# Token sums and residual of a down projection, moved from VectorE and GpSimd to accumulating DMA

## The chip, the cores and the metric

The kernel runs on one core of one Trainium2 chip. The core has a matrix engine (PE), three elementwise engines (DVE, ACT, POOL), a queue engine (SP) and 16 DMA engines. The metric is the device time of one launch in microseconds. Plain loads and stores are issued from SP; transfers that add into their destination ("accumulating DMA") are issued from POOL.

## The reference, cut to what matters

A decoder trunk of two layers over 1024 tokens, model width 1024, everything in float32. Both layers end in a gated feed-forward block, and the change touches only that block's second half:

```python
def swiglu(h, w_gu, w_down):
    u = h @ w_gu
    g, v = u[..., :D_FF], u[..., D_FF:]          # D_FF = 2816
    return (jax.nn.silu(g) * v) @ w_down

h = h + swiglu(rmsnorm(h, norm_g[layer, 1]), ffn_w_gu[layer], ffn_w_down[layer])
```

The first layer's output feeds a key/value projection, the last layer's a final RMSNorm.

## The kernel before, in words

**Layout.** Activations lie transposed: model or hidden dimension in 128 partitions, the 1024 tokens along the row. A tile is 128x1024, "lo" is tokens 0 to 511 and "hi" tokens 512 to 1023. All large tiles come from one pool of 49 slots. A float32 product is made of three matmuls on split operands: ACT copies the operand to a rounded high part (`split`, L229) and DVE subtracts to get the low part (L230). Both parts share one tile, `so`.

**Down.** `ffn` writes 22 gated tiles `t1` to DRAM (`zd`). `down` multiplies them with the weights `w_dn` in `block_proj`, in three groups of 3, 4 and 4 pairs of tiles (`DG`). Inside a group the product of 2x2 blocks (two halves of the hidden dimension by two halves of the tokens) is done with seven block products instead of eight, as in Strassen's method. They are named j and run in the order 1, 5, 6, 3, 7, 4, 2; each has four output tiles p, and one (j, p) is 3 matmuls per pair of tiles: 9 in the first group, 12 in the others. A j is called a phase here, so a phase is 48 matmuls in groups two and three.

The operand X of a phase (`xop`, four tiles k in groups two and three) is a sum of quarters of the two stored tiles a = `raw[k]` and b = `raw[G+k]`. Before, the chain of sums runs in place on POOL: phase 5 takes a.hi - a.lo (L939), phase 6 takes b.hi minus that (L945), phase 7 a.hi - b.hi (L941), phase 4 takes b.lo minus the sum of phase 6 (L943). Each sum is then split by ACT and DVE into an `so` tile; phases 1 and 3 are split with a sign (L948, L949). The operand of the next phase is written into the program after the present phase's product of the same index.

The weights need such sums as well; those were already made by accumulating DMA (`acc`, L188, tile `wr`), each after the split that reads the old content.

Results leave PSUM (tiles pU, pV, pW) by a DVE add or subtract into the residual tiles `h` (L1018). These are loaded at the start of `down` from the DRAM copy `hd` with eight plain loads of 512 KB (L858).

**Order.** Apart from the recurrent layer, a scheduler sets the order of each engine's queue when the program is built; at run time every queue is strictly in order. Weight work runs ahead of the products by a fixed number of steps (`SLA` = 6 for splits, four more for the loads and sums).

Of the kernel before, what the change touches and what calls it, by code (L numbers as in the profile page):

```python
# [9 lines left out]
AF = mybir.ActivationFunctionType  # L10
ALU = mybir.AluOpType
# [4 lines left out]
KD = 8  # L16
# [3 lines left out]
DG = [3, 4, 4]  # L20
# [47 lines left out]
class Trunk:  # L68
# [602 lines left out]
    def ffn(self, L, h, last=False):  # L671
        nc = self.nc
        zd = self.dram(f"zd{L}", [FF_T, P, S])
        lo, hi = slice(0, 512), slice(512, 1024)
# [78 lines left out]

        banks, tmp = {}, {}

        def product(i):
            f, j = seq[i]
            bank, xn = prod[j]
            if (f, bank) not in banks:
                banks[(f, bank)] = self.ps("p" + bank)  # L760
            p = banks[(f, bank)]
            w = ops.pop((f, j))
            for k in range(4):
                wh, wl = w[:, k * P:(k + 1) * P], w[:, 512 + k * P:512 + (k + 1) * P]
                xh, xl = X[xn][k][:, lo], X[xn][k][:, hi]
                for n, (a, b) in enumerate(((wh, xh), (wh, xl), (wl, xh))):
                    nc.tensor.matmul(p, a, b, start=k + n == 0 and j in (1, 5, 6), stop=k == 3 and n == 2,  # L767
                                     skip_group_check=j not in (1, 5, 6))
# [3 lines left out]
        def evict(f, j):  # L772
            a, b, c = (banks.get((f, x)) for x in "abc")
            if j == 1:
                t0, t1, t2 = tmp[f] = [self.slot("ev") for _ in range(3)]
                nc.scalar.activation(t0[:, lo], a, AF.Copy)  # L776
                return
            t0, t1, t2 = tmp[f]
            rb = st.get("rb")
            if j == 6:  # L780
                V(t0[:, hi], t0[:, lo], b, ALU.subtract)
            elif j == 2:
                V(t2[:, lo], a, rb[:, lo], ALU.mult)
                nc.scalar.activation(t2[:, lo], t2[:, lo], AF.Silu)
                nc.gpsimd.tensor_tensor(t2[:, lo], t2[:, lo], rb[:, lo], ALU.mult)
            elif j == 7:
                V(t1[:, hi], b, t0[:, lo], ALU.subtract)
                V(t1[:, hi], t1[:, hi], c, ALU.add)
            elif j == 4:
                V(t1[:, lo], b, t0[:, lo], ALU.subtract)  # L790
                V(t1[:, lo], t1[:, lo], t2[:, lo], ALU.mult)
            elif j == 3:
                V(t0[:, hi], t0[:, hi], c, ALU.subtract)  # L793
                nc.gpsimd.tensor_tensor(t0[:, hi], t0[:, hi], rb[:, hi], ALU.mult)  # L794
                nc.scalar.activation(t0[:, hi], t0[:, hi], AF.Silu)  # L795
                nc.gpsimd.tensor_tensor(t0[:, hi], t0[:, hi], rb[:, hi], ALU.mult)
                V(t1[:, hi], t1[:, hi], t0[:, hi], ALU.mult)
                zout.append((f, t1))
                for x in "abc":
                    del banks[(f, x)]  # L800
                del tmp[f]
# [41 lines left out]
    def down(self, L, hd, zd, zout, last):  # L843
        nc = self.nc
        self.ld = 4
        for x in zout:
            nc.sync.dma_start(zd[x[0]], x[1])
        zout.clear()
        h = [None] * KD

        def zload(f):
            t = self.slot("zr")
            nc.sync.dma_start(t, zd[f])
            return t

        def hload(m):
            h[m] = self.slot("h")
            nc.sync.dma_start(h[m], hd[m])  # L858

        k0 = [2 * sum(DG[:g]) for g in range(len(DG))]  # L860
        pr = self.block_proj(h, hload, DG, [lambda k, g=g: zload(k0[g] + k) for g in range(len(DG))],
                             [f"d{L}_{g}" for g in range(len(DG))], [self.d["w_dn"][L, g] for g in range(len(DG))],
                             (1, 5, 6, 3, 7, 4, 2), last)
        next(pr)
        yield
        next(pr)
        yield
        next(pr)
        yield
        if last:  # L870
            st = {}

            def sq(m, c, eng):
                n = c.stop - c.start
                if c.start not in st:
# [12 lines left out]
        for j, p, c in pr:  # L888
            if last:
                for m, x in {3: ((p, hi),), 7: ((p + 4, hi),), 4: ((p + 4, q[0]), (p + 4, q[1]))}.get(j, ((p, c),) if c else ()):  # L890
                    with self.tc.high_priority(offset=PRIO if j == 2 else 0):
                        sq(m, x, nc.vector if j == 2 else nc.gpsimd)
                if (j, p) == (7, 3):
                    fin = self.finish(h, st.pop(512), 512, 512)
                if j == 4 or c == q[0]:
                    next(fin, None)
                if (j, p, c) == (2, 3, q[0]):
                    for _ in fin:
                        pass
                    fin = self.finish(h, st.pop(0), 0, 256)  # L900
                    with self.tc.high_priority(offset=PRIO):
                        next(fin)
            else:
                for m, x in {3: ((p, hi),), 7: ((p + 4, hi),), 4: ((p + 4, lo),), 2: ((p, lo),)}.get(j, ()):
                    kv(m, x)
                if (j, p) == (4, 3):
                    self.ld, self.sp = LD, SP
                    self.wpump(self.wi + 4, self.wi + 2)
        if last:
            next(fin)  # L910
            next(fin)
            f1 = self.finish(h, st.pop(256), 256, 256)
            with self.tc.high_priority(offset=PRIO):
                next(f1)
            for f in (fin, f1):
                for _ in f:
                    pass
            yield h
        else:
            yield kv  # L920

    def block_proj(self, h, hload, G, xload, wkey, wsrcs, order, tail=False):
        nc = self.nc
        V = nc.vector.tensor_tensor
        lo, hi = slice(0, 512), slice(512, 1024)
# [9 lines left out]
        def xop(g, j, k):  # L935
            a, b = xraw(g, k), xraw(g, G[g] + k)
            t = self.slot("so", F32R)
            if j == 5:
                nc.gpsimd.tensor_tensor(a[:, lo], a[:, hi], a[:, lo], ALU.subtract)  # L939
            elif j == 6:  # L940
                nc.gpsimd.tensor_tensor(a[:, lo], b[:, hi], a[:, lo], ALU.subtract)  # L941
            elif j == 4:
                nc.gpsimd.tensor_tensor(a[:, lo], b[:, lo], a[:, lo], ALU.subtract)  # L943
            elif j == 7:
                nc.gpsimd.tensor_tensor(a[:, hi], a[:, hi], b[:, hi], ALU.subtract)  # L945
            x = {1: a[:, lo], 2: b[:, lo], 5: a[:, lo], 6: a[:, lo], 3: b[:, hi], 7: a[:, hi], 4: a[:, lo]}[j]
            if j in (1, 3):
                nc.scalar.activation(t[:, lo], x, AF.Copy, scale=-1.0)  # L948
                nc.vector.scalar_tensor_tensor(t[:, hi], x, -1.0, t[:, lo].bitcast(F32),  # L949
                                               op0=ALU.mult, op1=ALU.subtract)  # L950
            else:
                self.split(t[:, lo], t[:, hi], x)
            X.setdefault((g, j), []).append(t)
            if j == order[6]:
                raw[g][k] = raw[g][G[g] + k] = None
# [44 lines left out]
        def product(i, c0=0, c1=512):  # L1000
# [14 lines left out]
            m += p  # L1015
            c = slice(c.start + c0, c.start + c1)
            with self.tc.high_priority(offset=PRIO if c1 - c0 < 512 else 0):
                V(h[m][:, c], h[m][:, c], ps, op)  # L1018
            if c1 < 512:
                return  # L1020
            del ops[i]
# [2 lines left out]
            if p == 3:  # L1024
                del X[(g, j)]

        moves = {1: (0, lo, ALU.subtract), 2: (0, lo, ALU.add), 5: (4, hi, ALU.add), 6: (0, hi, ALU.subtract),
                 3: (0, hi, ALU.subtract), 7: (4, hi, ALU.add), 4: (4, lo, ALU.add)}

# [17 lines left out]
        for i in range(len(seq)):  # L1047
# [4 lines left out]
            if tail and i >= len(seq) - 4:  # L1052
                product(i, 0, 256)
                yield j, p, slice(0, 256)
                continue
            product(i)
            ng, nj = (g, order[o + 1]) if o < 6 else (g + 1, order[0])
            if ng < len(G) and p < G[ng]:
                xop(ng, nj, p)
# [913 lines left out]
```

## Time and profile before

| | us |
|---|---|
| three runs | 2746.46, 2748.12, 2750.28 |
| the profiled execution, launch to end | 2747.98 |
| its span, first to last instruction | 2746.2 |
| PE busy in the span | 2660.8 (97%) |
| down of layer one, first to last product | 911.2 to 1134.4 |
| down of layer two, first product starts at | 2497.5 |

The profiled execution lies 0.14 us under the median of the runs, and 1.8 us of it lie outside the span. PE is busy nearly all the time at a granted clock of 0.985, so only the idle stretches of PE can be won without changing its work, and anything that makes PE wait is lost directly. In views by stretch, each engine's busy time and, in brackets, its instructions stand beside the granted clock, the busy share of the DMA engines and what they moved. A share a little over 1 is possible, since packets overlap.

### The profile page before, as it was taken

Reading aid. Unit: us, or ns where it says so; the run is one execution under the profiler, and the core shown is the slowest. Engines: PE = TensorE matmul, PEld = TensorE weight load, DVE = VectorE, ACT = ScalarE, POOL = GpSimd, SP = SyncE. Lnnn points to the kernel's source line nnn. Section 1 sums busy time; section 2 is a strip of 40 time slices with the busy share of each in tenths; the row PEclk is TensorE's granted clock in tenths of the full one; section 3 lists DMA queues with packets and bytes.
Section 4 is the critical chain, followed back from the end, with each engine's and each line's share of the span. In section 5 each row is a group of like instructions: output and inputs, shape, how many; then the busy total and the mean of one; then the engine's idle time right before and its main releaser. Section 6 shows DMA issues by size and latency. Waiting matters only on the chain.

```text
span 2746.2 us, 36684 instructions
## 1 busy us (share of the span) xinstructions
PE 2660.8 (97%) x12650; PEld 2207.8 (80%) x12650; DVE 1893.9 (69%) x3641; ACT 1294.6 (47%) x2500; POOL 1117.1 (41%) x1102
## 2 busy tenths in 40 slices
PE   8889999999999999999999999999999999999997
PEld 6668888788888788888888888888887888887786
DVE  7667533755555798647647999999856655557997
ACT  4667222432232443424515788999934323223433
POOL 1441002544343555110004677777734434336552
PEclk9989999999999999999999999999999999999998
DMA  3334243476664976352485322221254666659761
GB/s 121 91 99 151 98 152 102 106 176 152 163 150 116 311 200 137 130 153 84 163 240 158 82 68 66 66 67 58 95 182 104 168 161 150 150 134 280 195 150 62
DMA packets 175178, 377.03 MB, mean 137 GB/s; under 512 B 16896, under 2 KB 66432, under 8 KB 174992
## 3 DMA queue, kind: packets, MB, share of 16 engines
q1 hardware_dynamic: 121232, 256.79, 29.1%
q0 software_dynamic: 51872, 115.43, 20.1%
q8 instruction: 100, 1.64, 0.3%
q10 hardware_dynamic: 1888, 2.46, 0.3%
q14 instruction: 86, 0.70, 0.1%
HBM read 289.68 MB, written 78.64 MB: 134 GB/s over the span
## 4 chain that ended last, share of the span: by engine, by line
PE 59%; DVE 11%; issue 4%; DMA 3%; ACT 3%; POOL 1%; DVEq 0%; POOLq 0%; ACTq 0%
PE pb L767 12%; PE pc L767 8%; PE pa L767 7%; PE pn L237 7%; PE pU L1012 5%; PE psc L237 4%; PE pV L1012 3%; PE pt L1634 3%; DVE so L230 2%; DMA wr<-w_dn 2%; PE pwo L1824 2%; PE po L1672 1%; PE po L1673 1%; PE pW L1012 1%; DVE thl L230 1%
## 5 line engine op out<-in xcount | busy, mean ns | idle before, releaser
L230 DVE TENSOR_TENSOR so<-wr,so 128x512 fp32r<-128x512 f32 (+1 forms) x476 | 387.1, 842 | 58.5 <-ACT so L229 57.9
L229 ACT ACTIVATE so<-wr 128x512 fp32r<-128x512 f32 (+1 forms) x476 | 279.1, 611 | 255.4 <-DMA wr<-w_dn 115.1
L767 PE MATMUL pb<-so,so 128*128 128x512 f32 x1584 | 381.1, 391 | 1.9 <-DVE so L230 1.4
L767 PEld LDWEIGHTS pb<-so,so 128*128 128x128 f32 x1584 | 298.4, 189 | 64.9 <-DVE so L230 1.8
L767 PE MATMUL pa<-so,so 128*128 128x512 f32 x1056 | 254.4, 393 | 3.6 <-ACT ev L776 2.4
L767 PE MATMUL pc<-so,so 128*128 128x512 f32 x1056 | 255.6, 389 | 0.0
L188 POOL DMA_DIRECT2D wr<-w_gu x176 | 161.6, 1077 | 226.2 <-DVE so L230 177.1
L1012 PE MATMUL pU<-so,so 128*128 128x512 f32 x1056 | 245.3, 390 | 2.3 <-DVE so L230 2.3
L767 PEld LDWEIGHTS pa<-so,so 128*128 128x128 f32 x1056 | 199.9, 190 | 46.2 <-ACT ev L776 2.5
L237 PE MATMUL psc<-kl,ql 96*128 96x512 f32 (+2 forms) x960 | 234.6, 370 | 2.0 <-DVE thl L230 1.2
L1012 PEld LDWEIGHTS pU<-so,so 128*128 128x128 f32 x1056 | 197.8, 188 | 45.2 <-DVE so L230 3.9
L767 PEld LDWEIGHTS pc<-so,so 128*128 128x128 f32 x1056 | 198.3, 188 | 41.1
L795 ACT ACTIVATE ev<-ev 128x512 f32<-128x512 f32 x44 | 27.8, 633 | 345.7 <-POOL ev L794 345.7
L237 PEld LDWEIGHTS psc<-kl,ql 96*128 96x128 f32 x960 | 165.7, 192 | 24.4 <-PE pt L1634 2.3
L188 POOL DMA_DIRECT2D wr<-w_dn x96 | 92.3, 1145 | 137.4 <-DVE so L230 67.6
L794 POOL TENSOR_TENSOR ev<-ev,rb 128x512 f32<-128x512 f32 x44 | 58.1, 1321 | 208.0 <-DVE ev L793 208.0
L230 DVE TENSOR_TENSOR thl<-pt,thl 128x512 fp32r<-128x512 f32 x198 | 133.0, 680 | 9.9 <-ACT thl L229 9.7
L1012 PE MATMUL pV<-so,so 128*128 128x512 f32 x528 | 125.9, 395 | 8.1 <-DVE so L230 6.9
L230 DVE TENSOR_TENSOR wl<-wr,wh 128x1024 fp32r<-128x1024 f32 (+4 forms) x79 | 89.2, 1145 | 55.1 <-ACT wh L229 31.2
L1012 PEld LDWEIGHTS pV<-so,so 128*128 128x128 f32 x528 | 99.5, 190 | 32.6 <-DVE so L230 8.8
L229 ACT ACTIVATE wh<-wr 128x1024 fp32r<-128x1024 f32 (+4 forms) x97 | 90.4, 956 | 74.0 <-DMA wr<-w_q 19.0
L229 ACT ACTIVATE thl<-pt 128x512 fp32r<-128x512 f32 x198 | 114.6, 598 | 21.1 <-PE pt L1634 19.3
(331 smaller groups left out, 6366.2 us busy)
## 6 DMA issues: line engine op xcount, KB each, us to landing
wr<-w_gu SPq DMA_DIRECT2D x110, 512.0 KB, 5.0
wr<-w_gu POOLq DMA_DIRECT2D x176, 256.0 KB, 5.2
zd<-ev SPq DMA_DIRECT2D x44, 512.0 KB, 3.2
zr<-zd SPq DMA_DIRECT2D x44, 512.0 KB, 6.3
wr<-w_dn SPq DMA_DIRECT2D x40, 512.0 KB, 7.2
wr<-w_dn POOLq DMA_DIRECT2D x64, 256.0 KB, 5.6
ql<-qd SPq DMA_DIRECT2D x64, 192.0 KB, 3.0
wr<-w_in SPq DMA_DIRECT2D x23, 512.0 KB, 4.3
```

Of the source, the lines that this page charges most:

```text
L188: self.nc.gpsimd.dma_start(dst, src, accum_op=ALU.add)
L229: nc.scalar.activation(hi, src, AF.Copy)
L230: (nc.gpsimd if pool else nc.vector).tensor_tensor(lo, src, hi.bitcast(F32), ALU.subtract)
L237: self.nc.tensor.matmul(ps, a, b, start=j == 0, stop=j == n - 1)
L767: nc.tensor.matmul(p, a, b, start=k + n == 0 and j in (1, 5, 6), stop=k == 3 and n == 2, skip_group_check=j not in (1, 5, 6))
L794: nc.gpsimd.tensor_tensor(t0[:, hi], t0[:, hi], rb[:, hi], ALU.mult)
L795: nc.scalar.activation(t0[:, hi], t0[:, hi], AF.Silu)
L1012: nc.tensor.matmul(ps, a, b, start=k + n == 0 and j in (1, 5, 2), stop=k == G[g] - 1 and n == 2, skip_group_check=j not in (1, 5, 2))
L1634: nc.tensor.transpose(pt[:, h * P:(h + 1) * P], Pt[n][h][r][:, off:off + P], self.ident)
L1672: nc.tensor.matmul(po[n], v, thl[:, 0:512], start=False, stop=False)
L1673: nc.tensor.matmul(po[n], v, thl[:, 512:1024], start=False, stop=end)
L1824: self.nc.tensor.matmul(p, wk[a], x[b], start=k + j == 0, stop=k == KD - 1 and j == 2)
```

## The change

1. The four results that are the first to reach a quarter of `h` (phases 1, 5, 6 and 4 of the first group, 16 products per layer) are copied out of PSUM by ACT with the right sign, instead of being added by DVE to a loaded residual. The eight loads of `hd` go away.
2. The residual is added in the second group by 16 accumulating DMAs of 256 KB from `hd` into `h`, written into the program after the products of phases 6, 3, 4 and 2.
3. `ffn` stores its gated tiles with signs chosen so that every sum of `xop` is a plain addition. Two evictions per tile swap operands or an add for a subtract; their number is the same.
4. The token sums are then accumulating DMAs from `zd` into the loaded tile, each issued after the split that reads the old content. In groups two and three all four sums of a pair are DMAs. In the first group those of phases 5 and 6 stay on POOL and two are DMAs. Per layer, 44 POOL sums become 6, and 38 accumulating DMAs of 256 KB are added.

```diff
         def hload(m):
             h[m] = self.slot("h")
-            nc.sync.dma_start(h[m], hd[m])
+
+        def hadd(m, c):
+            self.acc(h[m][:, c], hd[m][:, c])
...
             t = self.slot("so", F32R)
-            if j == 5:
-                nc.gpsimd.tensor_tensor(a[:, lo], a[:, hi], a[:, lo], ALU.subtract)
-            elif j == 6:
-                nc.gpsimd.tensor_tensor(a[:, lo], b[:, hi], a[:, lo], ALU.subtract)
-            elif j == 4:
-                nc.gpsimd.tensor_tensor(a[:, lo], b[:, lo], a[:, lo], ALU.subtract)
-            elif j == 7:
-                nc.gpsimd.tensor_tensor(a[:, hi], a[:, hi], b[:, hi], ALU.subtract)
-            x = {1: a[:, lo], 2: b[:, lo], 5: a[:, lo], 6: a[:, lo], 3: b[:, hi], 7: a[:, hi], 4: a[:, lo]}[j]
-            if j in (1, 3):
+            s, c = {1: (a, lo), 2: (b, lo), 3: (b, hi), 7: (a, hi)}.get(j, (a, lo))
+            x = s[:, c]
+            if g == 0 and j in (5, 6):
+                nc.gpsimd.tensor_tensor(x, x, (a if j == 5 else b)[:, hi], ALU.add)
+            if j == 6:
                 nc.scalar.activation(t[:, lo], x, AF.Copy, scale=-1.0)
...
+            sa, sb = xsrc[g](k), xsrc[g](G[g] + k)
+            if j == 1 and g:
+                self.acc(a[:, lo], sa[:, hi])
+                self.acc(a[:, hi], sb[:, hi])
+            elif j == 5:
+                self.acc(a[:, hi if g == 0 else lo], sb[:, hi])
+            elif j == 6:
+                self.acc(a[:, lo], sb[:, lo])
...
-                V(h[m][:, c], h[m][:, c], ps, op)
+                if (m, c.start) in fresh:
+                    fresh.remove((m, c.start))
+                    nc.scalar.activation(h[m][:, c], ps, AF.Copy, scale=-1.0 if op == ALU.subtract else 1.0)
+                else:
+                    V(h[m][:, c], h[m][:, c], ps, op)
...
+        adds = {(1, 6): (0, lo), (1, 3): (4, lo), (1, 4): (0, hi), (1, 2): (4, hi)}
...
             product(i)
+            if (g, j) in adds:
+                m, c = adds[(g, j)]
+                hadd(m + p, c)
```

The scheduler then orders three queues otherwise, in both layers alike. In the rows below `zr` is a loaded gated tile, `wr` a weight tile.

On SP, at the start of down of layer one, before:

```order
L853 DMA zr_6267<-zd_2929 128x1024
L853 DMA zr_6334<-zd_2929 128x1024
L858 DMA h_6339<-hd_2552 128x1024
L858 DMA h_6341<-hd_2552 128x1024
L858 DMA h_6343<-hd_2552 128x1024
L858 DMA h_6345<-hd_2552 128x1024
L183 DMA wr_6351<-w_dn 128x2x384
L838 DMA zd_2929<-ev_6037 128x1024
```

and now:

```order
L866 DMA zr_6267<-zd_2929 128x1024
L866 DMA zr_6334<-zd_2929 128x1024
L183 DMA wr_6347<-w_dn 128x2x384
L851 DMA zd_2929<-ev_6037 128x1024
L851 DMA zd_2929<-ev_6165 128x1024
```

Nothing stands between the tile loads and the next weight load any more.

On ACT, in the first group (from the weights of phase 5 on), before:

```order
L229 ACTIVATE so_6379<-zr_6256 128x512
L229 ACTIVATE so_6386<-wr_6192 128x384
L229 ACTIVATE so_6400<-zr_6258 128x512
L229 ACTIVATE so_6407<-wr_6192 128x384
L229 ACTIVATE so_6421<-zr_6260 128x512
L795 ACTIVATE ev_6164<-ev_6164 128x512
L229 ACTIVATE so_6428<-wr_6190 128x384
L229 ACTIVATE so_6443<-wr_6190 128x384
```

and now:

```order
L1039 ACTIVATE h_6339<-pU_6363 128x512
L229 ACTIVATE so_6374<-zr_6256 128x512
L229 ACTIVATE so_6381<-wr_6192 128x384
L1039 ACTIVATE h_6340<-pU_6384 128x512
L229 ACTIVATE so_6395<-zr_6258 128x512
L229 ACTIVATE so_6402<-wr_6192 128x384
L1039 ACTIVATE h_6341<-pU_6405 128x512
L229 ACTIVATE so_6416<-zr_6260 128x512
L229 ACTIVATE so_6423<-wr_6190 128x384
L808 ACTIVATE ev_6164<-ev_6164 128x512
L1039 ACTIVATE h_6342<-pU_6426 128x512
```

The copies out of PSUM, each of which waits for its product, stand between the splits.

On POOL, at the start of the second group, before:

```order
L945 TENSOR_TENSOR zr_6668<-zr_6668,zr_6710 128x512
L188 DMA wr_6838<-w_dn 128x512
L945 TENSOR_TENSOR zr_6670<-zr_6670,zr_6712 128x512
L188 DMA wr_6749<-w_dn 128x512
L939 TENSOR_TENSOR zr_6691<-zr_6691 128x512
L188 DMA wr_6749<-w_dn 128x512
L945 TENSOR_TENSOR zr_6689<-zr_6689,zr_6727 128x512
L941 TENSOR_TENSOR zr_6668<-zr_6710,zr_6668 128x512
```

and now:

```order
L188 DMA zr_6684<-zd_2929 128x512
L188 DMA zr_6662<-zd_2929 128x512
L188 DMA wr_6741<-w_dn 128x512 x2
L188 DMA zr_6664<-zd_2929 128x512
L188 DMA h_6354<-hd_2552 128x512
L188 DMA wr_6759<-w_dn 128x512 x2
L188 DMA zr_6682<-zd_2929 128x512
L188 DMA wr_6777<-w_dn 128x512
L188 DMA h_6379<-hd_2552 128x512
L188 DMA wr_6792<-w_dn 128x512
L188 DMA h_6400<-hd_2552 128x512
```

The queue now holds only transfers, those of the residual among those of weights and token sums.

More of the change, by code (lines that the diff above doesn't have):

```diff
@@ L754, in ffn, with first_half @@
         banks, tmp = {}, {}
+        def first_half(f):
+            for n in DG:
+                if f < 2 * n:
+                    return f < n
+                f -= 2 * n
         def product(i):
@@ L786, in evict @@
             elif j == 7:
-                V(t1[:, hi], b, t0[:, lo], ALU.subtract)
-                V(t1[:, hi], t1[:, hi], c, ALU.add)
+                if first_half(f):
+                    V(t1[:, hi], b, t0[:, lo], ALU.subtract)
+                    V(t1[:, hi], t1[:, hi], c, ALU.add)
+                else:
+                    V(t1[:, hi], t0[:, lo], b, ALU.subtract)
+                    V(t1[:, hi], t1[:, hi], c, ALU.subtract)
             elif j == 4:
-                V(t1[:, lo], b, t0[:, lo], ALU.subtract)
+                if first_half(f):
+                    V(t1[:, lo], t0[:, lo], b, ALU.subtract)
+                else:
+                    V(t1[:, lo], b, t0[:, lo], ALU.subtract)
                 V(t1[:, lo], t1[:, lo], t2[:, lo], ALU.mult)
@@ L857, in hload @@
             h[m] = self.slot("h")
-            nc.sync.dma_start(h[m], hd[m])
+        def hadd(m, c):
+            self.acc(h[m][:, c], hd[m][:, c])
         k0 = [2 * sum(DG[:g]) for g in range(len(DG))]
         pr = self.block_proj(h, hload, DG, [lambda k, g=g: zload(k0[g] + k) for g in range(len(DG))],
+                             [lambda k, g=g: zd[k0[g] + k] for g in range(len(DG))],
                              [f"d{L}_{g}" for g in range(len(DG))], [self.d["w_dn"][L, g] for g in range(len(DG))],
-                             (1, 5, 6, 3, 7, 4, 2), last)
+                             (1, 5, 6, 3, 7, 4, 2), hadd, last)
         next(pr)
@@ L920, in down, with block_proj @@
             yield kv
-    def block_proj(self, h, hload, G, xload, wkey, wsrcs, order, tail=False):
+    def block_proj(self, h, hload, G, xload, xsrc, wkey, wsrcs, order, hadd, tail=False):
         nc = self.nc
@@ L1017, in product @@
             with self.tc.high_priority(offset=PRIO if c1 - c0 < 512 else 0):
-                V(h[m][:, c], h[m][:, c], ps, op)
+                if (m, c.start) in fresh:
+                    fresh.remove((m, c.start))
+                    nc.scalar.activation(h[m][:, c], ps, AF.Copy, scale=-1.0 if op == ALU.subtract else 1.0)
+                else:
+                    V(h[m][:, c], h[m][:, c], ps, op)
             if c1 < 512:
@@ L1025, in product @@
                 del X[(g, j)]
+        fresh = {(m, c0) for m in range(KD) for c0 in (0, 512)}
+        adds = {(1, 6): (0, lo), (1, 3): (4, lo), (1, 4): (0, hi), (1, 2): (4, hi)}
         moves = {1: (0, lo, ALU.subtract), 2: (0, lo, ALU.add), 5: (4, hi, ALU.add), 6: (0, hi, ALU.subtract),
```

## The prediction

> **What bounds the kernel now.** First the page's line of engines: PE is busy 97% of the span, so the question is what its idle time in down waits for. Then PE's waits in the two down stages (columns: who, for what, us in total, times, longest), layer one and layer two:
>
> ```profile
> PE 2660.8 (97%) x12650; PEld 2207.8 (80%) x12650; DVE 1893.9 (69%) x3641; ACT 1294.6 (47%) x2500; POOL 1117.1 (41%) x1102
> ```
> ```profile
> PE pV L1012 <- DVE so L230: 3.5, 2, 2.3
> PE pU L1012 <- DVE so L230: 1.0, 2, 0.7
> PE pV L1012 <- ACT so L948: 0.3, 1, 0.3
> ```
> ```profile
> PE pV L1012 <- DVE so L230: 3.4, 2, 2.0
> PE pU L1012 <- DVE so L230: 1.3, 2, 0.7
> PE pV L1012 <- ACT so L948: 0.7, 1, 0.7
> PE pV L1012 <- ACT so L229: 0.2, 1, 0.2
> ```
>
> That is 4.8 us and 5.6 us: 10.4 us, 0.38% of the time, is all that down can give back. No matmul is added or removed. The timeline of PE in layer one says where the waits lie (start, length, work, and in brackets the idle time before it):
>
> ```profile
> 928.84 8.49 PE L1012 MATMUL pV<-so,so 128*128 128x512 f32 x29 [2.25 <-DVE so L230]
> 938.72 7.82 PE L1012 MATMUL pU<-so,so 128*128 128x512 f32 x33 [0.70 <-DVE so L230]
> ...
> 979.91 11.04 PE L1012 MATMUL pU<-so,so 128*128 128x512 f32 x48
> 990.79 2.43 PE L1012 MATMUL pV<-so,so 128*128 128x512 f32 x10
> 994.45 8.95 PE L1012 MATMUL pV<-so,so 128*128 128x512 f32 x38 [1.23 <-DVE so L230]
> 1003.24 2.43 PE L1012 MATMUL pU<-so,so 128*128 128x512 f32 x10
> 1005.95 4.37 PE L1012 MATMUL pU<-so,so 128*128 128x512 f32 x18 [0.28 <-DVE so L230]
> ```
>
> With the 0.3 us on L948, 3.3 us are lost in the first group and 1.5 us in the second, whose phases 1, 5 and 6 start at 979.91, 990.79 and 1003.24. A phase of 48 matmuls takes 990.79 - 979.91 = 10.9 us. The third group waits for nothing.
>
> PE waits for splits by DVE. The row of the stretch 905 to 1095 (us; PE, PEld, DVE, ACT, POOL busy; clock; DMA share; GB/s) shows DVE nearly full, and the groups of that stretch show why:
>
> ```profile
> 905.00:1095.00 190.00, 185.20 (x804) 151.08 (x803) 172.42 (x217) 78.68 (x143) 106.27 (x93) 0.99 0.80 213
> ```
> ```profile
> L230 DVE TENSOR_TENSOR so<-wr,so 128x512 fp32r<-128x512 f32 x46 | 56.0, 1216 | 1.3 <-ACT so L229 1.2
> L230 DVE TENSOR_TENSOR so<-zr,so 128x512 fp32r<-128x512 f32 x44 | 40.2, 913 | 0.0
> L1018 DVE TENSOR_TENSOR h<-h,pU 128x512 f32<-128x512 f32 x40 | 26.7, 677 | 3.0 <-PE pU L1012 3.0
> L949 DVE SCALAR_TENSOR_TENSOR so<-zr,so 128x512 fp32r<-128x512 f32 x22 | 18.1, 823 | 1.2 <-ACT so L948 1.1
> ...
> L188 POOL DMA_DIRECT2D wr<-w_dn x44 | 41.9, 1074 | 59.0 <-DVE so L230 32.5 <-PE pU L1012 26.5
> L945 POOL TENSOR_TENSOR zr<-zr,zr 128x512 f32<-128x512 f32 x11 | 20.3, 1851 | 1.4 <-DMA zr<-zd 1.4
> L939 POOL TENSOR_TENSOR zr<-zr 128x512 f32<-128x512 f32 x11 | 18.8, 1706 | 1.3 <-DVE so L949 1.0
> ```
> ```profile
> L1018 DVE TENSOR_TENSOR h<-h,pU x96: 669/675/689, 925.5 to 2710.9; 128x512 f32<-128x512 f32 x96
> L949 DVE SCALAR_TENSOR_TENSOR so<-zr,so x44: 676/682/6095, 905.6 to 2667.6; 128x512 fp32r<-128x512 f32 x44
> ```
>
> The last two rows give minimum, median and maximum in ns. A DVE operation with one operand in PSUM (L1018) never takes more than 0.69 us. One of the same size with both operands in SBUF takes 0.68 us in the median but up to 6.1 us, and the means of the splits are 1.22, 0.91 and 0.82 us: they stall beside POOL's sums, which take 1.7 to 1.9 us.
>
> The other resource is DMA. Rows: queue, packets, MB, share of the 16 engines; and issues with their median us to landing. In order, the stretches 895 to 1100, 1040 to 1046, 955 to 965 and 905 to 915:
>
> ```profile
> q1 hardware_dynamic: 12659, 31.99, 43.3%
> q0 software_dynamic: 7029, 11.74, 35.8%
> zr<-zd SPq DMA_DIRECT2D x22, 512.0 KB, 5.5
> ...
> h<-hd SPq DMA_DIRECT2D x8, 512.0 KB, 14.4
> ```
> ```profile
> q0 software_dynamic: 603, 1.11, 105.5%
> wr<-w_dn POOLq DMA_DIRECT2D x2, 256.0 KB, 9.0
> ```
> ```profile
> q1 hardware_dynamic: 1374, 3.65, 97.2%
> wr<-w_dn SPq DMA_DIRECT2D x6, 512.0 KB, 7.2
> zr<-zd SPq DMA_DIRECT2D x3, 512.0 KB, 4.4
> ```
> ```profile
> q1 hardware_dynamic: 631, 2.27, 60.5%
> q0 software_dynamic: 612, 0.84, 48.3%
> wr<-w_dn POOLq DMA_DIRECT2D x2, 192.0 KB, 15.4
> ```
>
> q0 holds the accumulating transfers, q1 the plain ones. Alone and saturated, q0 moves 1.11 MB in 6 us and q1 3.65 MB in 10 us, so 256 KB accumulated (0.262 MB) take 1.42 us and 512 KB loaded (0.524 MB) 1.44 us. In the mixed stretch these prices make 4.5 + 6.2 = 10.8 us for 10 us: both are 8% high, and I use 1.31 and 1.33 us. Accumulating a byte costs the engines twice what loading it costs.
>
> **The change, part by part (per layer).**
>
> *Eight residual loads go.* 8 x 1.33 = 10.6 us of DMA time leave the start of down, where landings took 14.4 us, and eight issues leave SP, so the next weight load stands higher. The chain of waits there is a weight sum that lands late:
>
> ```profile
> 903.14 12.79 DMA wr<-w_dn
> ```
>
> It feeds the splits that PE waits for at 928.84. I expect the first group's 3.3 us back, from both the earlier landing and a freer DVE.
>
> *Sixteen results copied by ACT.* The nearest row is ACT's read of a PSUM tile of the same size:
>
> ```profile
> L229 ACT ACTIVATE thl<-pt 128x512 fp32r<-128x512 f32 x198 | 114.6, 598 | 21.1 <-PE pt L1634 19.3
> ```
>
> 16 x 0.60 = 9.6 us on ACT, which is busy 79 of 190 us; 16 x 0.675 = 10.8 us leave DVE. Each copy waits for its product, and the splits behind it wait too. By the order of ACT these are the weights of the sixth product ahead and the operand of the phase after the running one; the third operand of a phase then has one product, 9 x 0.227 = 2.0 us, in hand for its split of 1.28, so I cost this at nothing. Without that cover it would be 0.6 us for each of the four copies of a phase, 2.4 us.
>
> *Thirty-eight POOL sums go.* DVE's excess over 0.68 us is 46 x 0.54 + 44 x 0.23 + 22 x 0.14 = 38 us. With the copies, DVE falls from 172 to about 124 of 190 us, and its waits in the second group (1.5 us) lose their cause. Whether a DMA issue on POOL stalls DVE too isn't separated by a row; between nothing and the sums' effect I take nothing, since the longest stalls lie beside sums. POOL itself gains little: 54 issues of 1.07 us replace 38 sums of about 1.7.
>
> *Sums and residual by DMA.* 38 + 16 transfers of 1.31 us are 70.7 us of DMA time. From 895 to 1100 the engines have 140 us of work now (11.74 and 31.99 MB at the prices above); with 70.7 more and 10.6 less it is 200 of 205 us. So DMA becomes full, and the question is when the operands land. Tightest is the second group's phase 6, since its operand needs two sums in a row on the same tile. In POOL's order, 30 transfers run from the group's first sum to the last of those: 12 token sums, 12 weight sums, 6 of the residual. They can start when the first tile has landed. SP's timeline:
>
> ```profile
> 944.52 12.54 SPq L853 DMA_DIRECT2D zr<-zd  x8
> ```
>
> A tile lands 5.5 us after its issue (median of the `zr` row above), so at 950, and the first sum can start at 951. With the 9 loads of the stretch 955 to 965 in the way: 951 + 30 x 1.31 + 9 x 1.33 = 1002.3, and 0.60 + 0.68 for the split: 1003.6. PE needs this operand 9 matmuls into phase 6, 9 x 0.227 = 2.0 us after its start, today at 1005.3. If the 4.5 us before it (3.3 + 1.2) come back, PE is there at 1000.7 and waits 2.9 us. So layer one gains 4.8 - 2.9 = 1.9 us, layer two by the same wait 5.6 - 2.9 = 2.7 us. Bounds: no wait if the sums find gaps (gain 4.8), and at the unrounded 1.42 and 1.44 us a landing 4.3 us later, so a wait of 7.2 us (loss 2.4).
>
> By the Trainium skill, page "DMA: Bandwidth & Descriptors", section "Anatomy of one DMA — SWDGE (gpsimd) path", a transfer issued by POOL takes about 2 us plus its bytes over 436 GB/s. That page has no price for one that accumulates; by its rate 256 KB would be 0.6 us, the 54 transfers 32 us, and DMA would not bind at all (the cover case below). The trace disagrees: 1.42 us at saturation.
>
> In the third group PE waits for nothing today, and no residual goes out; I cost it at nothing, the cover being the operands that are made ahead. Without it, the second group's wait would come once more. The first group's two sums per pair are needed in phases 7 and 4, two phases later: nothing. The signs in `ffn` swap operands of the same instructions: nothing. The tail after the last product is untouched.
>
> *Sum.* 1.9 + 2.7 = 4.6 us. The profiled execution of 2747.98 us, which is the median of the runs to 0.14 us, becomes 2743.4.
>
> **Rivals.**
>
> *Cover holds.* All sums land in time and every wait on DVE goes: 2747.98 - 10.4 = 2737.6. For it: nearly all of PE's waits end on DVE, which falls to two thirds. Against it: 200 us of work for 205 in DMA.
>
> *DMA is late (the other side).* Where both queues are full a sum of 192 KB landed after 15.4 us, and one of 256 KB after 9.0 us where only q0 was. One link from an operand to the next is split 1.28, issue 1.07 and landing; with 9.0 it is 11.4 us, with 15.4 it is 17.8, against a phase of 10.9 us. It decides from a landing of 8.5 us on. At 15.4 the second group's two links lose 2 x 6.9 = 13.8 us per layer, net of the gains 9.0 and 8.2: 2765. The residual's transfers, in line between the sums and held until ACT has copied, make it worse: the weight sums behind them wait, and PE for those. For it: all 16 residual transfers fall into the second group. Against it: a late PE eases the load at once. The Trainium skill, page "DMA: Bandwidth & Descriptors", section "SWDGE vs HWDGE vs iDMA", says that an engine takes turns between the two kinds of queue; by that a sum beside loads runs at half rate, 2 x 1.31 us, as in this case. The row of 905 to 915 agrees: 0.84 MB of sums, not 1.85.
>
> *Nothing changes.* The gain in the first group is real but DVE and DMA swap places in the second, and the wait there equals the gain: 2748. That is a wait of 5 us, between the sum's 2.9 and its bound of 7.2.
>
> **How the numbers follow.** A measurement here tells about 0.2%, 5.5 us, from no change: faster is below 2742.6, slower above 2753.6. The sum's case (2739.5 to 2746) has 0.35, cover 0.27, nothing changes 0.12, late DMA 0.26. Faster: cover and a third of the sum's case, 0.39. Slower: 0.25 of the late case. Same: the rest, 0.36. The likeliest is the sum's, 2743.4, on its own 2739 to 2747. The range takes in cover at the low end, and at the high end landings of up to about 14.7 us: 2737 to 2762.
>
> **What would show it.** Right: DVE's mean for `so<-wr` falls to about 0.7 us and its busy share in down to two thirds; PE's waits on DVE in the first group vanish; the DMA share over the stage rises to nearly 1; a wait of some 3 us appears at the start of the second group's phase 6, released by the split of a `zr` whose sum came late. Wrong: `so<-wr` stays above 1 us (then issues stall DVE as sums do); the waits in the first group stay (then neither the residual loads nor DVE made them, or ACT's copies hold the splits back); waits of over 5 us in phases 5 and 6, or any on weights in the third group (then DMA binds harder than I price it).

## The result, and the profile after

| | before | after |
|---|---|---|
| median of four runs on the same chip, us | 2748.6 (2746.46 to 2750.28) | 2781.92 (2778.93 to 2783.34) |
| ratio, 95% interval | | 1.0120 (1.0108 to 1.0132) |
| span of the profiled execution, us | 2746.2 | 2779.7 |
| waits of PE in down, layers one and two, us | 4.8 + 5.6 | 18.6 + 14.6 |
| PE busy, us, over the same 12650 matmuls | 2660.8 | 2673.6 |

The change costs 33 us, where a gain of 4.6 was forecast. The two lower rows hold it: PE waits 22.8 us more, and takes 12.8 us more for the same matmuls. The page's line of engines, then PE's waits in the two down stages:

```profile
PE 2673.6 (96%) x12650; PEld 2217.2 (80%) x12650; DVE 1810.5 (65%) x3609; ACT 1311.6 (47%) x2532; POOL 1103.8 (40%) x1134
```
```profile
PE pV L1031 <- ACT so L229: 13.9, 4, 8.2
PE pU L1031 <- DVE h L1041: 3.1, 1, 3.1
PE pV L1031 <- DVE so L230: 1.4, 3, 0.8
PE pU L1031 <- DVE so L960: 0.2, 1, 0.2
```
```profile
PE pV L1031 <- ACT so L229: 11.2, 3, 5.0
PE pU L1031 <- ACT so L959: 2.3, 1, 2.3
PE pV L1031 <- DVE so L230: 0.9, 2, 0.7
PE pU L1031 <- DVE so L960: 0.2, 1, 0.2
```

The waits on DVE have shrunk, and ACT's splits have taken their place. PE's timeline in layer one shows where:

```profile
943.23 9.40 PE L1031 MATMUL pV<-so,so 128*128 128x512 f32 x33 [2.87 <-ACT so L229]
...
998.27 11.28 PE L1031 MATMUL pV<-so,so 128*128 128x512 f32 x39 [8.24 <-ACT so L229]
...
1082.32 0.50 PE L1031 MATMUL pV<-so,so 128*128 128x512 f32 x1 [2.07 <-ACT so L229]
...
1095.08 12.56 PE L1031 MATMUL pU<-so,so 128*128 128x512 f32 x48 [3.10 <-DVE h L1041]
```

These are phase 3 of the first group, phase 5 of the second (its fourth operand, after nine matmuls), and phases 5 and 6 of the third. The last one is put down to an eviction by DVE, which stands in DVE's queue behind splits that wait 0.6 to 1.9 us each for ACT. ACT isn't busy there. Its timeline before 998:

```profile
983.32 0.63 ACT L229 ACTIVATE so<-zr 128x512 fp32r<-128x512 f32 x1 [0.67 <-DMA zr<-zd]
995.52 0.63 ACT L229 ACTIVATE so<-wr 128x512 fp32r<-128x512 f32 x1 [11.57 <-DMA wr<-w_dn]
997.59 0.63 ACT L229 ACTIVATE so<-zr 128x512 fp32r<-128x512 f32 x1 [1.44 <-DMA zr<-zd]
```

ACT stands 11.57 us for a weight sum and 1.44 us for a token sum, both accumulating DMAs. That token sum was issued at 983.81, so it landed after 13.8 us. In the chain of waits from 955.72 to 1005.53 us (start, length, what) four transfers fill 46.4 of 49.8 us, one behind the other:

```profile
955.72 11.98 DMA wr<-w_dn
...
970.13 10.58 DMA wr<-w_dn
...
981.22 12.26 DMA h<-hd
...
993.99 11.54 DMA zr<-zd
```

The row of 895 to 1095 (columns as before), the splits on DVE, and the queues and issues of 895 to 1100:

```profile
895.00:1095.00 200.00, 181.51 (x774) 146.76 (x772) 121.84 (x186) 79.97 (x147) 101.56 (x111) 0.97 1.05 258
```
```profile
L230 DVE TENSOR_TENSOR so<-zr,so 128x512 fp32r<-128x512 f32 x50 | 38.6, 772 | 4.6 <-ACT so L229 4.5
L230 DVE TENSOR_TENSOR so<-wr,so 128x512 fp32r<-128x512 f32 x44 | 30.3, 693 | 47.1 <-ACT so L229 47.1
```
```profile
q0 software_dynamic: 14207, 24.84, 67.6%
q1 hardware_dynamic: 11426, 27.67, 37.4%
...
wr<-w_dn SPq DMA_DIRECT2D x20, 512.0 KB, 12.9
zr<-zd POOLq DMA_DIRECT2D x38, 256.0 KB, 10.5
wr<-w_dn POOLq DMA_DIRECT2D x32, 256.0 KB, 11.1
h<-hd POOLq DMA_DIRECT2D x16, 256.0 KB, 11.3
```

DVE was relieved as forecast: `so<-wr` fell from 1216 to 693 ns, and DVE now idles 47.1 us on ACT. DMA is full: 1.05 of the stretch. A weight load lands after 12.9 us and a sum of 256 KB after 10.5 to 11.3 us.

### The profile page after: what moved, and what is told of

The parts are those of the page before. It is cut to its first block, busy times and chain, and to the rows that moved or that the text cites. A ratio compares the mean times of both kernels' runs of the same rounds, so it can differ in the third digit from the quotient of the medians.

```text
span 2779.7 us, 36781 instructions
## 1 busy us (share of the span) xinstructions
PE 2673.6 (96%) x12650; PEld 2217.2 (80%) x12650; DVE 1810.5 (65%) x3609; ACT 1311.6 (47%) x2532; POOL 1103.8 (40%) x1134
## 4 chain that ended last, share of the span: by engine, by line
PE 54%; DVE 9%; DMA 9%; issue 4%; ACT 3%; POOL 2%; POOLq 0%; DVEq 0%; SPq 0%; ACTq 0%
PE pb L773 11%; PE pc L773 7%; PE pa L773 7%; PE pn L237 6%; DMA wr<-w_dn 6%; PE psc L237 4%; PE pU L1031 3%; PE pt L1662 3%; PE pV L1031 2%; DMA zr<-zd 2%; PE pwo L1852 2%; PE po L1700 1%; PE po L1701 1%; DVE so L230 1%; DVE thl L230 1%
## 5 line engine op out<-in xcount | busy, mean ns | idle before, releaser
L230 DVE TENSOR_TENSOR so<-wr,so 128x512 fp32r<-128x512 f32 (+1 forms) x476 | 341.7, 748 | 159.7 <-ACT so L229 159.3
L1031 PE MATMUL pV<-so,so 128*128 128x512 f32 x528 | 134.9, 413 | 27.4 <-ACT so L229 25.1
L188 POOL DMA_DIRECT2D wr<-w_dn x96 | 98.1, 1198 | 75.5 <-DMA wr<-w_dn 33.4
L188 POOL DMA_DIRECT2D zr<-zd x76 | 84.6, 1143 | 100.2 <-DMA zr<-zd 34.7
## 6 DMA issues: line engine op xcount, KB each, us to landing
zr<-zd POOLq DMA_DIRECT2D x76, 256.0 KB, 10.3
```

The source lines that it names most:

```text
L188: self.nc.gpsimd.dma_start(dst, src, accum_op=ALU.add)
L230: (nc.gpsimd if pool else nc.vector).tensor_tensor(lo, src, hi.bitcast(F32), ALU.subtract)
L1031: nc.tensor.matmul(ps, a, b, start=k + n == 0 and j in (1, 5, 2), stop=k == G[g] - 1 and n == 2, skip_group_check=j not in (1, 5, 2))
```

## The experiments

All kernels are made from the changed one. `D` lists the phases whose token sums are transfers, by group; the rest of the sums are POOL additions. The changed kernel is `D = [(7, 4), (5, 6, 7, 4), (5, 6, 7, 4)]`:

```diff
-            if g == 0 and j in (5, 6):
+            if j in (5, 6, 7, 4) and j not in D[g]:
                 nc.gpsimd.tensor_tensor(x, x, (...)[:, ...], ALU.add)
...
-            if j == 1 and g:
+            if j == 1 and 5 in D[g]:
                 self.acc(a[:, lo], sa[:, hi])
...
```

"Residual as before" means eight loads of `hd` and DVE's adds. The table gives the ratio to the kernel before with its interval; PE's idle time in down of layer one before products; DMA's busy share from 905 to 1115 us; and the median time in us from issue to landing of the token sums. Each kernel was timed against 4 to 25 runs of the kernel before on its chip (medians 2746.4 to 2748.6 us).

| | ratio | PE waits | DMA share | landing |
|---|---|---|---|---|
| before | 1 | 4.8 | 0.73 | |
| changed | 1.0120 (1.0108, 1.0132) | 18.6 | 1.00 | 10.5 |
| 1 residual part alone | 1.0027 (1.0018, 1.0037) | 7.8 | 0.78 | |
| 2 token sums alone | 1.0077 (1.0062, 1.0092) | 11.3 | 0.95 | 9.8 |
| 3 without residual transfers | 1.0024 (1.0013, 1.0035) | 7.4 | 0.90 | 9.9 |
| 4 phases 5 and 6 on POOL | 1.0020 (1.0011, 1.0030) | 8.1 | 0.90 | 10.3 |
| 5 early half of the residual transfers in group three | 1.0128 (1.0113, 1.0143) | 18.7 | 1.01 | 9.8 |
| 6 all moved transfers at half width (and the gate and up weight sums) | 0.9970 (0.9956, 0.9984) | 2.2 | 0.85 | 7.3 |
| 7 residual transfers at half width | 1.0074 (1.0055, 1.0092) | 11.6 | 0.97 | 10.2 |
| 8 token sums at half width | 1.0009 (0.9999, 1.0019) | 7.5 | 0.91 | 9.0 |
| 9 as 1, early half of the transfers in group three | 1.0029 (1.0016, 1.0041) | 8.7 | 0.78 | |
| 10 as 1, no residual transfers | 0.9984 (0.9975, 0.9994) | 3.7 | 0.66 | |
| 11 as 1, transfers at half width | 1.0019 (1.0009, 1.0028) | 6.2 | 0.74 | |
| 12 sums of 7 and 4, groups two and three | 0.9983 (0.9974, 0.9992) | 3.4 | 0.81 | 9.2 |
| 13 sums of 5 and 6, groups two and three | 0.9996 (0.9987, 1.0006) | 6.2 | 0.79 | 9.6 |
| 14 all sums, groups two and three | 1.0017 (1.0008, 1.0026) | 4.7 | 0.91 | 9.7 |

### The halves of the change (1, 2, 3)

**1, the residual part alone.**

```diff
+ D = [(), (), ()]
```

> The residual part alone: ACT copies the sixteen first results, sixteen accumulating transfers bring the residual in the second group, all 44 token sums stay on POOL. Theory DMA (in the changed kernel the accumulating transfers, not the copies, make the operands late; 16 x 1.31 - 8 x 1.33 = 10 us more DMA work is far from filling the stage): within 0.3% of the kernel before, 2740 to 2752 us, no wait of PE over 4 us on ACT in down. Rival ACT (the copies wait for products and hold back the splits queued behind them): the loss stays, 2765 to 2782. Rival residual (the sixteen transfers, issued between the weight sums on POOL's queue, are what delays): also 2765 to 2782, but with PE's waits in the second group alone and ACT waiting for DMA on wr.

2753.3 us: a loss of 0.27%, 1 us above the range of the DMA theory and far under the others'. Taken up in 9 to 11.

**2, the token sums alone.**

```diff
+ nc.sync.dma_start(h[m], hd[m])     # in hload; no first copies, no hadd
```

> The token sums alone: 38 accumulating transfers from the stored tiles, residual loaded and added by DVE as before. Theory DMA: 38 x 1.31 = 50 us more work, 190 of the 205 us that the DMA engines have; sums still land after 8.5 us and PE still waits at phase 5 of the second and third group: 2760 to 2778 us. Rival residual: with the sixteen transfers gone the sums land in time, 2740 to 2752. Rival ACT: no copies, so no late splits, 2740 to 2752 as well, and the landing of zr sums may stay at 10 us without harm.

2768.5 us, as the DMA theory has it in size, but not in place. The largest wait is in the first group, and DVE makes it: it stands for residual loads that the token sums beside them made late (PE, then DVE):

```profile
942.47 9.70 PE L1032 MATMUL pU<-so,so 128*128 128x512 f32 x33 [7.25 <-DVE so L961]
```
```profile
934.45 0.69 DVE L1042 TENSOR_TENSOR h<-h,pV 128x512 f32<-128x512 f32 x1 [6.12 <-DMA h<-hd]
936.80 0.69 DVE L1042 TENSOR_TENSOR h<-h,pV 128x512 f32<-128x512 f32 x1 [1.66 <-DMA h<-hd]
```

**3, the changed kernel without residual transfers.**

```diff
- adds = {(1, 6): (0, lo), (1, 3): (4, lo), (1, 4): (0, hi), (1, 2): (4, hi)}
+ adds = {}
```

> The changed kernel without its sixteen residual transfers: the residual of the feed-forward blocks is left out of the computation. Copies by ACT and token sums by DMA stay. Theory DMA: 180 of 205 us, 21 us less than in the changed kernel; two thirds of its loss stay: 2760 to 2775 us, with waits at phase 5. Rival residual: 2738 to 2750. Rival ACT: 2775 to 2782, as changed.

2755.5 us, between the ranges of DMA and of the residual. Of the 33 us, 26 go with the sixteen residual transfers; yet where POOL makes the token sums (1 against 10 below) the same transfers cost 0.43%, 12 us. The parts are dear together, as they would be if something that they share filled up.

### Bytes, place or queue (4 to 8)

**4, the tight sums back on POOL.**

```diff
+ D = [(7, 4), (7, 4), (7, 4)]
```

> The changed kernel with the token sums of phases 5 and 6 on POOL in all three groups, as it has them in the first; those of phases 7 and 4, which are needed two phases after they are issued, stay transfers (22 instead of 38). Theory DMA, by links: a link of 1.28 + 1.07 + 10 to 11 us misses a phase of 10.9 us but not two phases, so PE waits no more than 2 us in the second and third group: 2740 to 2752 us. Rival, DMA full as such (weight sums late too): 22 + 16 transfers make 179 of 205 us, the waits on weights stay, 2755 to 2770. Rival ACT: 2765 to 2782.

2753.1 us, by 1 us outside the range of the links and below that of a full DMA. The largest wait, 4.83 us, is in phase 3 of the first group; the eight tile loads of the next group, which start at 938.10 where they started at 944.52 before, meet its weight sums (DMA share 1.06 from 935 to 955).

**5, the early half of the residual in the third group.**

```diff
+ adds = {(1, 4): (0, hi), (1, 2): (4, hi), (2, 1): (4, lo), (2, 5): (0, lo)}
```

> The changed kernel with its sixteen residual transfers 8 phases later: issued in the third group, not in the second. Theory place (the second group is where eight tile loads, the weights, their sums and the token sums meet; the third group has no tile loads behind it): PE's 8.2 us wait in phase 5 of the second group falls to 3 us or less as without residual transfers, the third group keeps its 5 us or gets some more: 2757 to 2770 us. Rival sum (only the total of 200 us counts): 2774 to 2784.

The edit moves eight of the sixteen transfers: those that stood after phases 6 and 3 of the second group (issued from 969.6 to 1008.0 us) now stand after phases 5 and 1 of the third; the eight after phases 4 and 2 stay. 2782 us, not a microsecond gained: the theory of the crowded second group falls. In phase 5 of the second group the 8.24 us fell to 1.27; the third group has them instead:

```profile
1085.46 11.62 PE L1031 MATMUL pV<-so,so 128*128 128x512 f32 x39 [10.57 <-ACT so L229]
```

**6, the same transfers with half the bytes.**

```diff
+ dst, src = dst[:, 0:256], src[:, 0:256]     # in acc, w_dn's sums excepted
```

> The changed kernel with its 38 token sums and 16 residual transfers per layer moved at half width: 256 of 512 columns, so half of each of these sums is left out of the computation. Number, order and place of the transfers stay. Theory capacity (the 16 DMA engines have too many bytes to move, so each sum waits its turn): the stage's DMA work falls from 200 to 165 us of 205, as low as in the kernels that lost 6 us: 2748 to 2758 us. Rival issue (not bytes, but the place in POOL's queue, the 1.07 us of an issue or the limit on transfers in flight holds them): 2774 to 2782, as the changed kernel.

2737.7 us, 10 us below the capacity theory's range. All loss goes, and a gain of 0.3% comes: in down no wait on DVE is left, and layer one loses 2.2 us in phase 3 of the first group:

```profile
940.52 2.61 PE L1033 MATMUL pV<-so,so 128*128 128x512 f32 x9 [1.65 <-ACT so L231]
943.70 5.74 PE L1033 MATMUL pV<-so,so 128*128 128x512 f32 x24 [0.57 <-ACT so L231]
```

The number of transfers is that of the changed kernel. Their order is so only nearly: 15 of the 102 accumulating transfers of down, per layer, stand elsewhere in POOL's queue (3 in 7 below, 10 in 8).

The edit also reaches further than was meant: it halves the 88 weight sums per layer that `ffn` makes before down. PE is busy without a break there with and without that (300 of 300 us from 600 to 900), and 42 of the 44 us between the profiled spans of this kernel and the changed one lie in the two down stages. So what costs is the bytes in down; 7 and 8, whose edits touch nothing else, confirm it. In the same stroke ACT's sixteen copies and the new signs, which this kernel has too, are shown to cost nothing that this gain doesn't cover.

**7 and 8, which bytes.** In 7 only `hadd` moves half, in 8 only the token sums do.

> The changed kernel with only its sixteen residual transfers at half width; half of the residual of the feed-forward blocks is left out of the computation, every issue stays. Without these transfers it took 2755.5 us, with them 2782. Theory bytes: half or more of the 26 us go, 2760 to 2771 us, since the DMA work falls from 220 to 208 us per layer. Rival place in the queue: 2775 to 2783.

> The changed kernel with only its 38 token sums at half width; half of each such sum is left out of the computation, every issue stays. Theory bytes: 220 - 38 x 0.73 = 192 us of DMA work per layer, about that of the kernel with everything at half width: 2738 to 2752 us. Rival place in the queue: 2775 to 2783.

2766.4 and 2748.3 us: bytes, both times. The recovery follows them. All bytes here are those moved in down. Per layer, 7 saves 16 x 0.131 = 2.1 MB, 8 saves 5.0, 6 saves 7.1; by the ratios (times 2747) the kernel gets 12.6, 30.5 and 41.2 us back over two layers, which is 3.0, 3.1 and 2.9 us for each MB, give or take 1.4, 0.4 and 0.4. Within these limits it doesn't matter whose bytes they are.

### The residual where DMA isn't full (9, 10, 11)

**9, as 1 with the early half of the transfers in the third group** (`D` of 1, `adds` of 5).

> Residual part alone with its sixteen transfers in the third group; token sums all on POOL. Against the residual part alone with transfers in the second group (2753.3 us). Theory place: the 3.6 us wait in phase 5 of the second group goes back to the 1.2 us of the kernel before, its loss shrinks to what the first group shows: 2746 to 2751. Rival ACT or early tile loads (the loss lies in the first group, where the eight tile loads now start at 939 instead of 944.5 us and land on the weight sums): 2751 to 2756, with the waits at 943 to 946 us unchanged.

2755.7 us, in the rival's range: nothing gained; phase 5 of the second group waits 0.99 us about as before the change, and phase 6 of the third waits 1.17 and 2.66. The loss moves with the transfers, so the rival's range was met, but not for its reason; 10 shows that the copies and the earlier tile loads don't make it.

**10, as 1 without the transfers** (`D` of 1, `adds` of 3).

> The residual part alone without its sixteen transfers: ACT copies the first results, all token sums on POOL, and the residual of the feed-forward blocks is left out of the computation. It shows what the copies and the freed loads do by themselves. If the copies cost nothing and the transfers' issues and bytes on POOL's queue made the 6.5 us loss of the residual part: 2736 to 2744 us. If the copies or the earlier tile loads made it: 2748 to 2756.

2743.5 us, 0.16% faster than before. The copies and the freed loads are a small gain, and the sixteen transfers the whole loss of 1.

**11, as 1 with the transfers at half width.**

```diff
+ c = slice(c.start, c.start + 256)     # in hadd
```

> The residual part alone (copies by ACT, token sums on POOL) with its sixteen transfers at half width: half of the residual of the feed-forward blocks is left out of the computation, the number of issues on POOL stays. Without these transfers the kernel took 2743.5 us, with them 2753.3. Theory bytes: half of the 10 us go, 2746 to 2749.5 us, and DMA's share between 955 and 1010 falls. Rival issue (each transfer stands in POOL's queue for 1.2 to 1.4 us between sums and weight sums, whatever it carries): 2751 to 2755.

2752.2 us: 0.35% of the 0.43% stay, so here the transfers cost mostly by standing in POOL's queue, whatever they carry. The intervals are about 0.1% wide on each side, so some share of bytes isn't excluded. The stretch 955 to 1010 (columns as before) in 1, in 11 and in 10:

```profile
955.00:1010.00 55.00, 51.40 (x220) 42.05 (x219) 55.00 (x60) 22.06 (x41) 43.08 (x40) 0.97 1.02 236
```
```profile
955.00:1010.00 55.00, 51.57 (x219) 41.65 (x218) 55.00 (x59) 23.56 (x44) 41.99 (x40) 0.97 0.94 215
```
```profile
955.00:1010.00 55.00, 54.89 (x242) 45.15 (x241) 55.00 (x65) 28.61 (x53) 36.29 (x32) 1.00 0.81 197
```

DVE (third pair) is full in all three, POOL (fifth) rises from 36 to 42 us with the issues, and beside POOL's sums DVE gets less done: 59 or 60 instructions instead of 65. No run separates the time of an issue from the delay of what stands behind it. PE pays in phase 5, here in 1:

```profile
993.14 10.53 PE L1033 MATMUL pV<-so,so 128*128 128x512 f32 x38 [3.60 <-DVE so L230]
```

### How much slack a sum needs (12, 13, 14)

**12, only the sums of phases 7 and 4, residual as before.**

```diff
+ D = [(), (7, 4), (7, 4)]
```

> The kernel before with only the sums of phases 7 and 4 of the second and third group as transfers (16 per layer, 21 us more DMA work, 161 of 205 us); first group and residual as before. Theory capacity with slack: two phases of time cover a landing of 10 us, DVE is stalled less, PE's 1.5 us of waits in the second group go, nothing comes in their place: 2742 to 2747 us. Rival: the sums push the weight sums late, PE waits on ACT's splits of weights: 2750 to 2757.

2741.7 us, 0.3 us below its range and 0.17% faster than before, with an interval that excludes 1: the one version that computes everything and beats both kernels. PE waits nowhere in groups two and three of layer one, and the first group is as it was. The stretch 955 to 1010:

```profile
955.00:1010.00 55.00, 55.00 (x244) 45.57 (x243) 48.73 (x70) 23.43 (x42) 32.60 (x32) 1.00 1.00 233
```

PE is busy all of it, and DVE 48.7 of 55 where it was full before.

**13, the sums of phases 5 and 6 instead** (`D = [(), (5, 6), (5, 6)]`).

> As the kernel that moved the sums of phases 7 and 4 of groups two and three (2741.7 us), but with those of phases 5 and 6 instead: the same sixteen transfers per layer, the same bytes, and half the slack or less, since each is issued after the split of one phase and needed in the next. Theory slack (a link of split, issue and landing, 1.28 + 1.07 + 9 us, against a phase of 10.9): PE waits 1 to 4 us at phases 5 and 6 of each of the two groups: 2748 to 2760 us. Rival bytes only: the same 2739 to 2745.

2746.4 us: the same bytes, no gain. It misses both ranges, between them. PE does not wait in phases 5 and 6 of the two groups, where theory slack said it would. In layer one it waits 1.25 us on an eviction by DVE in phase 4 of the second group, and in the first group 2.24 + 0.70 + 2.01.

**14, all four sums of groups two and three** (`D = [(), (5, 6, 7, 4), (5, 6, 7, 4)]`).

> All four token sums of groups two and three by transfer, those of the first group on POOL, residual as in the kernel before: 182 of 205 us of DMA work. Against the token sums alone (2768 us), which also had two transfers per pair in the first group. Theory crowding in the first group (those six transfers made the residual loads late, DVE stood 9 us for them, and PE 7.3): 2748 to 2758 us. Rival bytes in groups two and three: 2762 to 2770.

2752.6 us. The six transfers of the first group were what made 2 lose 16 us more. With 0.91 of DMA and landings of 9.7 us, PE's waits in layer one are all in the first group (layer two has one of 2.42 us more, in phase 6 of the second):

```profile
PE pV L1034 <- DVE so L230: 2.2, 1, 2.2
PE pV L1034 <- ACT so L229: 1.8, 1, 1.8
PE pU L1034 <- DVE so L962: 0.7, 1, 0.7
```

## Why the prediction was wrong, point by point

**The term that failed is the DMA work of the stage.** It was put at 140 us today and 200 with the change, of 205, from prices of queues that ran alone, cut by 8% to fit one mixed stretch. The rows for 895 to 1100 that stood beside it said otherwise: 43.3% and 35.8% of 205 us are 162. The same view from 895 to 1120, before and after:

```profile
q1 hardware_dynamic: 12667, 32.02, 39.5%
q0 software_dynamic: 7029, 11.74, 32.6%
```
```profile
q0 software_dynamic: 14694, 25.70, 63.7%
q1 hardware_dynamic: 11426, 27.67, 34.1%
```

Of 225 us that is 162 us of packet time before and 220 after. What the change adds was priced well: 58 us, where 60 were forecast (on q0 70.0 us for 13.96 MB more, 1.31 us for each 256 KB). The base was 22 us short, against a forecast gain of 4.6 in both layers. With 220 us for 205 the stage is 15 us over, where the prediction left 5 free. Down grew by 18.2 us in layer one and by 15.2 in layer two.

By this sum, q0 and q1 from 895 to 1120, the kernels that make token sums by DMA line up, but for 13:

| kernels | us of packet time | change in time |
|---|---|---|
| 13 | 175 | none |
| 12, 6 | 184, 194 | 0.2 and 0.3% faster |
| 3, 4, 8, 14 | 199 to 201 | 0.1 to 0.2% slower |
| 2, 7 | 209, 213 | 0.8 and 0.7% slower |
| changed, 5 | 220, 222 | 1.2 and 1.3% slower |

**The start of the sums.** They were to start at 951, and 30 transfers to run from there. POOL's timeline:

```profile
951.29 0.86 POOL L188 DMA_DIRECT2D zr<-zd  x1 [12.62 <-PE pV L1031]
...
966.60 0.86 POOL L188 DMA_DIRECT2D zr<-zd  x1 [10.51 <-DVE so L230]
...
983.81 0.86 POOL L188 DMA_DIRECT2D zr<-zd  x1 [0.42 <-issue]
```

Four sums start at 951; they are those for phase 7. The first for phase 5 writes the quarter that phase 1 reads, waits for that split, and goes at 966.60; the fourth goes at 983.81, behind weight sums and residual transfers. So the tight place was phase 5, not phase 6. The prediction's range took in landings of up to 14.7 us, and the 13.8 us that PE waited for in phase 5 lie inside it; but the range charged them to the second group alone.

**The third group** was costed at nothing and lost 5.2 us in layer one (2.07 and 3.10). Its cover is the same as the second group's, and DMA was full there too (a share of 1.11 from 1060 to 1100).

**The first group's 3.3 us** did come back as waits on DVE (the rows of 928.84 and 938.72 have no counterpart), but 2.87 us on ACT took their place, where a weight sum was late. Kernel 10 shows the same with POOL's sums: 0.98 on DVE and 2.72 on ACT. The next wait there is the weight chain's.

**The clock** was left out. PE's idle stretches cost twice: 12.8 us of the loss is slower matmuls, 12.3 of it in the products of down. A phase of 48 takes 11.04 us in the rows before and 12.56 at 1095.08, behind a wait of 3.10.

**Right:** ACT's copies and the signs at nothing (6, 10); DVE's excess gone, and DMA issues without sums beside them don't stall DVE (693 ns); DMA full; the cover case, had there been room: 2737.6 forecast, 2737.7 measured in 6, though the agreement to 0.1 us is luck (6 still waits 2.2 and 2.0 us in down, and the kernel before took 2746.9 beside it, not 2748.0).

The rival "DMA is late" had the mechanism and the waits of over 5 us, though its 2765 was still 17 us short. Its threshold, a landing of 8.5 us, is too low. In layer one, sums that land after 9.7 us (14) leave phases 5 and 6 of groups two and three without a wait; at 9.9 (3) the longest is 1.47 us, at 10.5 (the changed kernel) 8.24. But 5 has a median of 9.8 and a wait of 10.57. The threshold isn't a median landing; the operands of one phase are split one by one while the phase before runs.

The rule weighed in the prediction from the Trainium skill, page "DMA: Bandwidth & Descriptors", section "SWDGE vs HWDGE vs iDMA", that an engine takes turns between the two kinds of queue, fits the loads: weight loads on SP, fewer bytes than before, landed after 12.9 us with the sums beside them, and after 7.5 us in 12. No run tells that rule from engines that are simply full.

Open: whether plain loads taken away would have helped as much as sums taken away, byte for byte by their price; it wasn't tried. Why 13 gains nothing where 12 does is settled in part. Its sums of phases 7 and 4 stay on POOL; four of them run in a row from 1029.28 to 1036.23, four splits by DVE beside them take 1.2 to 1.8 us instead of 0.69, and the eviction behind them makes PE wait the 1.25 us. The 2.01 us on a weight sum in the first group, where 12 waits 0.49, stay open.

## What to carry to other kernels

Before work is moved to DMA, read from the queues' own shares of the busiest stretch what is used already, not from a queue's rate while it runs alone, and leave room. Of the kernels here that make token sums by DMA, those with a share of 0.81 and 0.85 gained (12, and 6, which leaves out half of each sum), those at 0.90 and 0.91 lost 0.1 to 0.2%, and 1.00 lost 1.2%. Room alone is no promise: 13 gained nothing at 0.79, and 1, 9 and 11 lost 0.2 to 0.3% at 0.74 to 0.78, where POOL's queue held transfers between sums.

Halving the bytes of a suspect transfer, with its issue left alone (6, 7, 8), tells capacity from queueing in one run; see to it that the edit halves nothing else. Try first the sums that have two phases of slack (12 gained, 13 didn't), and keep them out of a stretch whose loads are already late.

## What the runs showed of the hardware

- Accumulating costs the DMA engines about twice the packet time of loading per byte: 5.58 against 2.77 us per MB after the change (67.6% and 37.4% of 205 us for 24.84 and 27.67 MB, or 179 against 361 GB/s), 6.25 against 2.78 before it, and 5.4 against 2.7 us of time where each queue ran alone.
- A byte taken off the accumulating queue gives back about 3 us per MB of kernel time, the same within the intervals from 2 to 7 MB per layer, with DMA at 1.00 to 0.85. Where DMA isn't full it was less: in 11, at 0.74, 2.1 MB less per layer gave back 0.08%, within the noise.
- POOL has at most eight accumulating transfers under way, in the trace of every kernel here, the one before included. From 981.22 to 991.95 it issues eight; the ninth, at 993.99, goes half a microsecond after the first of them, a residual transfer into another tile, has landed at 993.48, and the trace gives that as its releaser. The traces also give POOL's transfers eight semaphores in turn (99 to 106), and the ninth takes over that of the first; so this may be a limit of the program, and whether the chip would hold more under way wasn't tried:

```profile
981.22 0.86 POOL L188 DMA_DIRECT2D h<-hd  x1 [0.64 <-DMA wr<-w_dn]
...
991.95 0.86 POOL L188 DMA_DIRECT2D wr<-w_dn  x1 [0.97 <-DMA wr<-w_dn]
993.99 0.86 POOL L188 DMA_DIRECT2D zr<-zd  x1 [1.18 <-DMA h<-hd]
```

  So where landings take 10.5 us, a transfer leaves every 1.3 us, and whatever stands in line delays what is behind it. Kernel 6, with nearly the same line, shows that the landings, and through them the line, hang on the bytes.
- A wait of PE costs clock on top. After 8.24 us of idle time the next 39 matmuls took 11.28 us, where 38 took 8.95 before the change. The granted clock (third from the end) around it:

```profile
990.00:1000.00 10.00, 1.76 (x4) 1.12 (x4) 1.50 (x3) 1.89 (x3) 4.64 (x6) 0.62 1.11 251
1000.00:1010.00 10.00, 10.00 (x40) 8.14 (x39) 6.39 (x10) 3.74 (x6) 6.67 (x9) 0.87 1.12 204
```

  In the middle, from 992.5 to 1002.5, it is 0.50, and before the change it is 0.51 from 930.5 to 933.5, just behind the wait of 2.25 us at 928.84. The extra 1.5 to 2.4 us hardly depend on the length of the wait: 3.10 us (48 matmuls in 12.56 for 11.04) costs nearly what 8.24 does, and 3.81 us in layer two costs the most (33 matmuls in 10.23, where 7.82 was usual):

```profile
2550.38 10.23 PE L1031 MATMUL pV<-so,so 128*128 128x512 f32 x33 [3.81 <-ACT so L229]
```

  The length of one wait doesn't tell whether it comes. After 2.07 us in layer one and 2.26 in layer two nothing slows, nor after 3.42 us in kernel 5; but 38 matmuls take 10.5 us instead of 8.9 after 1.80 us in 8, and after 0.75 and 1.47 us close together in 3. The Trainium skill, page "TensorE: Matmul & The Clock Gate", section "Part 1: The HAM clock gate (the "warmup" mystery)", has the clock halved after an idle window of about 3.4 us; the trace agrees on the half, though waits of 1.80 to 3.10 us were enough here.
